# A decoder block on one Trainium2 core: the up projection as Strassen's seven products, the down projection in two passes

## The chip, the cores and the metric

The kernel runs on one core of a Trainium2 chip. Five engines work side by side and meet at semaphores: TensorE (PE in the profile; its weight loads are listed as PEld), VectorE (DVE), ScalarE (ACT), GpSimd (POOL) and SyncE (SP), which here only issues DMAs. The metric is the device time of one execution in microseconds (us). Lower is better.

## The reference

One block, 512 tokens, width 2048, all in float32:

```python
h = _rmsnorm(x, norm1_g[l]) * (1.0 + sc1) + sh1
p = h @ w_in[l]
...
mix = jnp.concatenate([y_rwkv, y_pool], axis=-1) @ w_out[l]
x = x + gt1 * mix
h = _rmsnorm(x, norm2_g[l]) * (1.0 + sc2) + sh2
x = x + gt2 * _conv_ffn(h, w_up[l], conv_w[l], conv_b[l], w_down[l])
return _rmsnorm(x, norm_f_g)

def _conv_ffn(h, w_up, conv_w, conv_b, w_down):
    T = h.shape[1]
    u = h @ w_up
    up = jnp.pad(u, ((0, 0), (CONV_WIDTH - 1, 0), (0, 0)))
    y = conv_b
    for j in range(CONV_WIDTH):
        y = y + conv_w[j] * up[:, j:j + T]
    val, gate = jnp.split(y, 2, axis=-1)
    return (jax.nn.silu(gate) * val) @ w_down
```

y_rwkv is a recurrent mixer over 16 heads, y_pool a causal mean over 2 to 16 tokens; w_up is 2048 x 11264, w_down 5632 x 2048. The six vectors sh1 to gt2 come from `silu(c) @ w_ada + b_ada`. The change touches the feed-forward part and what stands just ahead of it.

## The kernel before, in words

Features lie on the 128 partitions and tokens along the free dimension, so a tile is 128 features x 512 tokens. D = 2048 is 16 tiles (KT), the feed-forward width 5632 is 44 tiles (NF) for the value and 44 for the gate.

Every large matrix product keeps float32 precision with three matmuls in a 32-bit reduced format. `split_weights` (L102) loads 128 x 512 weights (256 KB) into `wraw`, ScalarE casts them to `whi`, and VectorE subtracts to get the remainder `wlo`. Activations are split in the same way (`split_act`, `modulate`). `mm3` (L111) then multiplies hi x hi, hi x lo and lo x hi into the same PSUM bank, at L112, L113 and L114. `project` (L116) does that over all tiles of the contracted dimension. There are three `whi` and three `wlo` buffers and four `wraw`.

Stage A (L166 to L683) holds the first norm, the input projection, the mixers and the first blocks of the output projection. Stage B begins at L688. The output projection's last six outputs are computed in two halves of 256 tokens (`out_half`), so that the second norm of the first half (`norm_rows`, `norm_bcast`, `second_norm`) runs while TensorE works on the second. The first two pairs of up tiles are also done in halves (`up_first`, L731).

Then come six groups of 8, 8, 8, 8, 4 and 8 pairs (GROUPS). A pair is a value tile and a gate tile: two `up_tile` products of 16 k-tiles x 3 matmuls with 512 columns each, a convolution straight from PSUM (`conv`, L818: one ScalarE and two VectorE instructions), silu, product and split into A. After a group's pairs its part of the down projection follows: 16 outputs, each of which VectorE scales with the gate and adds to `x2` in SBUF (L848). The last group's outputs 8 to 15 are done in halves, so that the final norm of the first half and its store (`finish`, L862) lie beside the second. `ada_gate2` (L804) computes the last sixteenth of the modulation, gt2, on VectorE during the first group, in 64 instructions with a 256 KB load each.

The order on each engine is laid out ahead of time by a scheduler that follows the order of the program text as a priority and takes what is ready by its own model; on the chip each engine then runs its list in order. All DMAs stand in SP's queue. A buffer (a tag with `bufs` slots) is used again when its readers are done. `GROUPS`, `H2` (the 16 split tiles of the second norm), `x2` (16 tiles of the residual) and `actp` are the names that the change removes or moves.

Of the kernel before, what the change touches and what calls it, by code (L numbers as in the profile page):

```python
# [16 lines left out]
P = 128  # L17
# [37 lines left out]
def block_kernel(ctx, tc, a, out, stop=None, dbg=None):  # L55
# [4 lines left out]
    actp = ctx.enter_context(tc.tile_pool(name="act", bufs=1))  # L60
    wp = ctx.enter_context(tc.tile_pool(name="wts", bufs=2))
# [3 lines left out]
    cmat = cp.tile([P, 5, P], F32, tag="cmat", name="cmat")  # L65
    nc.sync.dma_start(cmat, a["cmat"][:, :, :])
    ident, bones, bmean, cent, ones = (cmat[:, i, :] for i in range(5))
    masks = cp.tile([P, 4, P], F32, tag="masks", name="masks")
    nc.sync.dma_start(masks, a["mask4"][:, :, :])
    mlev = cp.tile([P, 2, 64], F32, tag="mlev", name="mlev")  # L70
    nc.sync.dma_start(mlev, a["mlev"][:, :, :])
    scanm = cp.tile([P, NC, 129], F32, tag="scanm", name="scanm")
    nc.gpsimd.memset(scanm, 1.0)
    nc.gpsimd.memset(scanm[:, :, 0:1], 0.0)
    lanei = cp.tile([64, 16, 16], F32, tag="lanei", name="lanei")
    nc.sync.dma_start(lanei, a["lanei"][:, :, :])
    prec = cp.tile([P, 16], F32, tag="prec", name="prec")
# [33 lines left out]
    def mm3(ps, wh, wl, xh, xl, start, stop):  # L111
        PE.matmul(ps, wh, xh, start=start, stop=False)  # L112
        PE.matmul(ps, wh, xl, start=False, stop=False)  # L113
        return PE.matmul(ps, wl, xh, start=False, stop=stop)  # L114
# [575 lines left out]
    HT = T // 2  # L690

# [6 lines left out]

    def sumsq(acc, src, lo, hi, fresh):
        if fresh:  # L700
            S.activation(acc[:, lo:hi], src, AF.Square)
        else:
            t = rb.tile([P, T], F32, tag="h2", name="sqx", bufs=2)
            S.activation(t[:, lo:hi], src, AF.Square)
            V.tensor_add(acc[:, lo:hi], acc[:, lo:hi], t[:, lo:hi])

    H2 = [(rb.tile([P, T], F32R, tag=f"hh{k}", name=f"hh{k}"), rb.tile([P, T], F32R, tag=f"hl{k}", name=f"hl{k}"))
          for k in range(KT)]

    def residual(f, ps, gate, acc, lo, hi, fresh):  # L710

        V.scalar_tensor_tensor(x2[f][:, lo:hi], ps, gate, x2[f][:, lo:hi], op0=ALU.mult, op1=ALU.add)
        sumsq(acc, x2[f][:, lo:hi], lo, hi, fresh)
# [11 lines left out]
    def second_norm(hf, rstd, k):  # L725
        hs = slice(hf * HT, (hf + 1) * HT)
        t = rb.tile([P, T], F32, tag="h2", name="h2", bufs=2)[:, 0:HT]
        hi, lo = H2[k]
        modulate(hi[:, hs], lo[:, hs], t, x2[k][:, hs], rstd, gsc2[:, k : k + 1], mod[:, 48 + k : 49 + k])

    def up_first(hf, k):  # L731
        hs = slice(hf * HT, (hf + 1) * HT)
        wh, wl = split_weights(a["wup0"][k, :, :], G if hf == 0 and k % 2 else V)
        for i in range(4):
            sl = slice(i * P, (i + 1) * P)
            mm3(ups[i][:, hs], wh[:, sl], wl[:, sl], H2[k][0][:, hs], H2[k][1][:, hs], start=k == 0, stop=k == KT - 1)

    acc = rb.tile([P, T], F32, tag="acc", name="acc")
    x2 = []
# [12 lines left out]
    for f in range(8):
        residual(f, pss[f], mod[:, 32 + f : 33 + f], acc, 0, T, f == 0)
    for f in range(8, NW):
        ps = bank()
        project(ps, a["wout"][f, :, :], M)
        residual(f, ps, mod[:, 32 + f : 33 + f], acc, 0, T, False)

    def out_half(hf, f, engs=(V,)):
        ps = bank()[:, 0:HT]  # L760
        project(ps, a["wout"][f, :, :], half(M, hf), engs=engs)
        residual(f, ps, mod[:, 32 + f : 33 + f], acc, hf * HT, (hf + 1) * HT, False)

    for f in range(NW, KT):
        out_half(0, f)
    for f in range(NW, KT):
        if f == NW + 1:
            dg = norm_rows(acc[:, 0:HT])
        if f == NW + 2:
            rstd0 = norm_bcast(dg)  # L770
        if f >= NW + 2:
            for k in range(3 * (f - NW - 2), 3 * (f - NW - 1)):
                second_norm(0, rstd0, k)
        out_half(1, f, (V, G) if f >= NW + 2 else (V,))

    ups = [bank() for _ in range(4)]
    for k in range(KT):
        if k + 12 < KT:
            second_norm(0, rstd0, k + 12)
        if k == 2:  # L780
            dg = norm_rows(acc[:, HT:T])
        if k == 5:
            rstd = norm_bcast(dg)
        if k >= 5:
            for k_ in range((k - 5) * 2, min((k - 4) * 2, KT)):
                second_norm(1, rstd, k_)
        up_first(0, k)
    for k in range(KT):
        up_first(1, k)
# [4 lines left out]
    def slot(i, dt=F32):  # L794
        return actp.tile([P, T], dt, tag=f"a{'hl'[i // 16]}{i % 16}", name="slot")

    cbs = []
    for i in range(4):
        t = slot(8 + i)
        nc.sync.dma_start(t, cact[0:1, i * T : (i + 1) * T].partition_broadcast(P))  # L800
        cbs.append(t)
    modg = cp.tile([P, 4, KT], F32, tag="modg", name="modg")

    def ada_gate2(j, after):  # L804
        for kq in range(4):
            wa = slot(12 + (4 * j + kq) % 4)
            nc.sync.dma_start(wa, a["ada2"][kq, 48 + j, :, :])
            jk = slot(24 + (4 * j + kq) % 2)
            with tc.issue_after(after.ins):
                V.scalar_tensor_tensor(jk, wa, 1.0, cbs[kq], op0=ALU.mult, op1=ALU.mult,  # L810
                                       accum_out=modg[:, kq, j : j + 1])

    def up_tile(n):
        ps = bank()
        project(ps, a["wup"][n, :, :], H2)
        return ps

    def conv(ps, j, tag):  # L818
        y = rb.tile([P, T], F32, tag=tag, name=tag, bufs=2)
        S.activation(y, ps, AF.Identity, bias=col("cb", j), scale=col("cw", 176 + j))  # L820
        V.scalar_tensor_tensor(y[:, 1:T], ps[:, 0 : T - 1], col("cw", 88 + j), y[:, 1:T], op0=ALU.mult, op1=ALU.add)
        V.scalar_tensor_tensor(y[:, 2:T], ps[:, 0 : T - 2], col("cw", j), y[:, 2:T], op0=ALU.mult, op1=ALU.add)
        return y

    j0 = 0
    for gi, gn in enumerate(GROUPS):
        A = []
        for jj in range(gn):
            j = j0 + jj
            yv = conv(ups[2 * j] if j < 2 else up_tile(2 * j), j, "t0")  # L830
            yg = conv(ups[2 * j + 1] if j < 2 else up_tile(2 * j + 1), 44 + j, "t1")
            S.activation(yg, yg, AF.Silu)
            after = V.tensor_mul(yv, yv, yg)
            A.append(split_act(jj, yv))
            if gi == 0 and jj >= 4:
                for i in range(4 * (jj - 4), 4 * (jj - 3)):
                    ada_gate2(i, after)
        if gi == 0:
            V.tensor_add(modg[:, 0, :], modg[:, 0, :], modg[:, 1, :])
            V.tensor_add(modg[:, 2, :], modg[:, 2, :], modg[:, 3, :])  # L840
            V.tensor_add(modg[:, 0, :], modg[:, 0, :], modg[:, 2, :])
            V.tensor_add(mod[:, 80:96], modg[:, 0, :], cols("b_ada", 80, 96))
        wsrc = a["wdn"][:, :, j0 * P : (j0 + gn) * P]
        if gi < len(GROUPS) - 1:
            for f in range(KT):
                ps = bank()
                project(ps, wsrc[f], A)
                V.scalar_tensor_tensor(x2[f], ps, mod[:, 80 + f : 81 + f], x2[f], op0=ALU.mult, op1=ALU.add)  # L848
        else:

            acc = rb.tile([P, T], F32, tag="acc", name="acc")

            def gate(f):
                return mod[:, 80 + f : 81 + f]

            def down_half(hf, f):
                ps = bank()[:, 0:HT]
                project(ps, wsrc[f], half(A, hf))
                residual(f, ps, gate(f), acc, hf * HT, (hf + 1) * HT, False)

            def finish(hf, k, rstd):
                hs = slice(hf * HT, (hf + 1) * HT)  # L862
                V.scalar_tensor_tensor(x2[k][:, hs], x2[k][:, hs], col("nf", k), rstd, op0=ALU.mult, op1=ALU.mult)  # L863
                nc.sync.dma_start(out[:, k, hs], x2[k][:, hs])
# [119 lines left out]
```

## Time and profile before

| | us |
|---|---|
| median of 3 runs (lowest to highest) | 2449.82 (2446.82 to 2450.76) |
| the profiled execution | 2452.14 |
| its span, first to last instruction | 2450.0 |
| TensorE matmul busy in it | 2347.1 |
| VectorE busy | 1408.7 |
| ScalarE busy | 874.6 |
| GpSimd busy | 23.7 |

The profile is of one execution. "Busy" joins overlapping instructions of an engine. Matmuls are pipelined, and their listed durations overlap, so how many start in a stretch tells more than their busy time. A group's row has the line, engine, operation, tiles (out<-in), shapes and count; then busy time and mean ns of one; then the engine's idle time ahead of it and who ended that. In a windows row each engine has its busy time and, in brackets, its number of instructions; then follow the granted TensorE clock, the DMA engines' share and GB/s.

### The profile page before, as it was taken

What the parts mean: (1) busy time and instruction counts of PE and PEld (TensorE: products, weight loads), DVE (VectorE), ACT (ScalarE), POOL (GpSimd) and SP (SyncE); (2) the same over time, 40 slices, a digit from 0 to 9 for tenths busy, and PEclk for the clock granted to TensorE, in tenths of its full rate; (3) what the DMA queues carried; (4) which work ended last, traced back from release to release, by engine and by line L of the source; (5) the groups of instructions that cost most, each with busy time, mean ns of one, the idle gap of its engine ahead of it and who ended that gap; (6) DMA issues with size and microseconds to landing.
All of it is one profiled execution on the core that took longest, in us unless ns stands there. A gap on an engine that the chain in (4) does not pass through costs nothing.

```text
span 2450.0 us, 36089 instructions
## 1 busy us (share of the span) xinstructions
PE 2347.1 (96%) x13714; PEld 1872.0 (76%) x13714; DVE 1408.7 (57%) x2698; ACT 874.6 (36%) x1402; POOL 23.7 (1%) x29
## 2 busy tenths in 40 slices
PE   4889999999999999999999999999999999999997
PEld 3656666667667889887888888888888888888887
DVE  7987677787774357757534443444344434444457
ACT  3244443443433336532223322333233323323333
POOL 0000000000000002100000000000000000000000
PEclk9999999999999999999999999999999999999999
DMA  9975564556662635538533333333332333332335
GB/s 353 337 233 152 166 185 140 163 162 178 169 200 85 203 111 185 181 113 260 161 96 98 96 98 95 99 96 98 95 99 95 99 95 99 95 99 95 99 97 174
DMA packets 232160, 352.61 MB, mean 144 GB/s; under 512 B 74865, under 2 KB 80177, under 8 KB 227761
## 3 DMA queue, kind: packets, MB, share of 16 engines
q1 hardware_dynamic: 231986, 350.30, 46.0%
q8 instruction: 107, 1.75, 0.3%
q14 instruction: 67, 0.55, 0.1%
HBM read 334.22 MB, written 16.00 MB: 143 GB/s over the span
## 4 chain that ended last, share of the span: by engine, by line
PE 68%; DMA 3%; DVE 2%; ACT 1%; issue 0%; SPq 0%; POOL 0%; DVEq 0%; ACTq 0%; POOLq 0%
PE b L112 20%; PE b L114 20%; PE b L113 20%; DMA wraw<-wup 1%; PE mm L112 1%; PE mm L113 1%; PE mm L114 1%; DMA war<-ada 0%; PE pa L290 0%; DMA slot<-ada 0%; DMA wraw<-wdn 0%; DVE wlo L108 0%; DVE x L863 0%; PE pa L114 0%; PE pa L113 0%
## 5 line engine op out<-in xcount | busy, mean ns | idle before, releaser
L108 DVE TENSOR_TENSOR wlo<-wraw,whi 128x512 fp32r<-128x512 f32 x772 | 533.2, 692 | 694.9 <-ACT whi L106 679.6
L106 ACT CAST whi<-wraw 128x512 fp32r<-128x512 f32 x788 | 489.3, 622 | 1229.0 <-PE b L113 925.2
L114 PE MATMUL b<-hh,wlo 128*128 128x512 f32 (+1 forms) x1472 | 561.2, 381 | 5.9 <-DVE wlo L108 5.0
L112 PE MATMUL b<-hh,whi 128*128 128x512 f32 (+1 forms) x1472 | 560.0, 380 | 0.0
L113 PE MATMUL b<-hl,whi 128*128 128x512 f32 (+1 forms) x1472 | 559.5, 380 | 0.0
L112 PE MATMUL b<-ah,whi 128*128 128x512 f32 (+1 forms) x992 | 353.4, 357 | 4.3 <-ACT whi L106 2.5
L114 PE MATMUL b<-ah,wlo 128*128 128x512 f32 (+1 forms) x992 | 351.9, 355 | 0.8 <-DVE wlo L108 0.8
L113 PE MATMUL b<-al,whi 128*128 128x512 f32 (+1 forms) x992 | 352.1, 355 | 0.0
L114 PEld LDWEIGHTS b<-hh,wlo 128*128 128x128 f32 x1472 | 277.0, 188 | 62.1 <-DVE wlo L108 8.5
L112 PEld LDWEIGHTS b<-hh,whi 128*128 128x128 f32 x1472 | 276.9, 188 | 52.9 <-ACT whi L106 0.5
L113 PEld LDWEIGHTS b<-hl,whi 128*128 128x128 f32 x1472 | 277.0, 188 | 52.3
L112 PEld LDWEIGHTS b<-ah,whi 128*128 128x128 f32 x992 | 187.5, 189 | 33.7 <-ACT whi L106 4.3
L113 PEld LDWEIGHTS b<-al,whi 128*128 128x128 f32 x992 | 187.6, 189 | 27.4 <-DVE al L134 1.1
L114 PEld LDWEIGHTS b<-ah,wlo 128*128 128x128 f32 x992 | 187.6, 189 | 26.8 <-DVE wlo L108 1.2
L112 PE MATMUL mm<-ah,whi 128*128 128x512 f32 x464 | 192.4, 415 | 6.3 <-ACT upad L257 5.5
L113 PE MATMUL mm<-al,whi 128*128 128x512 f32 x464 | 191.8, 413 | 0.0
L114 PE MATMUL mm<-ah,wlo 128*128 128x512 f32 x464 | 190.1, 410 | 0.0
L343 DVE SCALAR_TENSOR_TENSOR jkr<-war,cq 128x512 bf16<-128x512 f32 x192 | 131.3, 684 | 18.7 <-DMA war<-ada 15.9
L848 DVE SCALAR_TENSOR_TENSOR x<-b,mod,x 128x512 f32<-128x512 f32 x80 | 59.7, 750 | 111.4 <-PE b L114 111.3
L112 PEld LDWEIGHTS mm<-ah,whi 128*128 128x128 f32 x464 | 88.4, 190 | 35.1 <-issue 10.4
L113 PEld LDWEIGHTS mm<-al,whi 128*128 128x128 f32 x464 | 88.3, 190 | 29.3 <-issue 13.0
L114 PEld LDWEIGHTS mm<-ah,wlo 128*128 128x128 f32 x464 | 88.4, 191 | 23.8 <-issue 6.3
(259 smaller groups left out, 2282.0 us busy)
## 6 DMA issues: line engine op xcount, KB each, us to landing
wraw<-wup SPq DMA_DIRECT2D x368, 256.0 KB, 3.0
war<-ada SPq DMA_DIRECT2D x192, 256.0 KB, 3.4
wraw<-wdn SPq DMA_DIRECT2D x192, 256.0 KB, 2.7
wraw<-win SPq DMA_DIRECT2D x140, 256.0 KB, 4.0
wa<-ada SPq DMA_DIRECT2D x32, 1024.0 KB, 6.9
wraw<-wout SPq DMA_DIRECT2D x88, 256.0 KB, 3.0
slot<-ada SPq DMA_DIRECT2D x64, 256.0 KB, 3.7
sp<-spill SPq DMA_DIRECT2D x21, 256.0 KB, 2.7
```

The lines of the kernel that those rows point to most:

```text
L106: S.copy(hi, raw)
L108: eng.tensor_tensor(lo, raw, hi[:, :].bitcast(F32), op=ALU.subtract)
L112: PE.matmul(ps, wh, xh, start=start, stop=False)
L113: PE.matmul(ps, wh, xl, start=False, stop=False)
L114: return PE.matmul(ps, wl, xh, start=False, stop=stop)
L343: V.scalar_tensor_tensor(jk, wa, 1.0, cq[0], op0=ALU.mult, op1=ALU.mult, accum_out=modq[:, kq, j : j + 1])
L848: V.scalar_tensor_tensor(x2[f], ps, mod[:, 80 + f : 81 + f], x2[f], op0=ALU.mult, op1=ALU.add)
```

## The change

The up projection is done by Winograd's form of Strassen's algorithm, one level deep. Weights of one pair are a 2 x 2 block matrix: value and gate (w11, w12 of the value, w21, w22 of the gate) by the lower and upper half of the 2048 inputs, each quarter 128 x 1024 as it lies in SBUF. Activations are a 2 x 2 block matrix of lower and upper features by first and second 256 tokens. Seven products of quarters, 8 k-tiles x 3 matmuls with 256 columns each, replace eight. Four weight sums r1 to r4 for each pair are made on VectorE, every quarter or sum is split by `wsplit` (one ScalarE cast and one VectorE subtraction of 128 x 1024), and results are put together from PSUM with three adds and some copies. The activation sums T1 to T4 and Y11, Y21, Y22 are made once (`normed`, `combos`, `split4`): steps 0 and 1 of `combos` make a half of T1 each, steps 2 and 3 a half of T2, T3 and Y22 each and leave T4's sum in t2's place, all from the second norm, which lies in the four 1 MB buffers x2_0 to x2_3. `combos(n - 1)` follows `first_two(n)` for n from 1 to 4; T4 is split after the fifth. The pairs' two weight rows of 1 MB then go into x2_0 to x2_3 in turn. Since the second half of the tokens is late, the two products that need only the first half (w11 and w12 of the value) are computed ahead for the first NB = 5 pairs (`first_two`); their weights are loaded again later.

The gated activations go to DRAM (`ad`). The down projection runs in two passes of 22 tiles over all 16 outputs; `act_pair` loads the activations of a pass and splits them into the buffers of Y11 to T4 as these come free; results of the first pass go to DRAM (`yd`) and come back with x2, which also waits in DRAM (`x2d`). In the second pass outputs 8 to 15 are in halves. `ada_gate2` becomes 16 instructions on 1 MB each, two for each of the first eight outputs of the first pass. GpSimd no longer takes part in the splits. Constants of the mixers, `wts` and `act` lie in pools on the right side of SBUF and are closed ahead of the up projection; the pool `ub` takes their place.

```diff
+    hctx = ExitStack()
+    tp = hctx.enter_context(tc.tile_pool(name="tables", bufs=1, side="right"))
+    wp = hctx.enter_context(tc.tile_pool(name="wts", bufs=2, side="right"))
+    actp = hctx.enter_context(tc.tile_pool(name="act", bufs=1, side="right"))
...
+    def wide(name):
+        return rb.tile([P, 4, HT], F32, tag="wide", name=name, bufs=3)
+    def quad(i, name, dt=F32):
+        return rb.tile([P, 4, T], dt, tag=f"x2_{i}", name=name)
...
+    def out_done(f, ps, lo, hi):
+        residual(f, ps, mod[:, 32 + f : 33 + f], acc, lo, hi, f == 0)
+        nc.sync.dma_start(x2d[f][:, lo:hi], x2(f, slice(lo, hi)))
...
+    def normed(q, hs, rstd):
+        t = wide("xr")
+        V.tensor_tensor(t, x2q[q][:, :, hs], rstd[:, None, :].to_broadcast([P, 4, HT]), op=ALU.mult)
+        for i in range(4):
+            f = 4 * q + i
+            S.activation(x2(f, hs), t[:, i, :], AF.Identity, bias=mod[:, 48 + f : 49 + f], scale=gsc2[:, f : f + 1])
+    def split4(pool, tag, src):
+        t = pool.tile([P, 2, 4, HT], F32R, tag=tag, name=tag)
+        S.copy(t[:, 0, :, :], src)
+        V.tensor_tensor(t[:, 1, :, :], src, t[:, 0, :, :].bitcast(F32), op=ALU.subtract)
...
+    ub = ctx.enter_context(tc.tile_pool(name="ub", bufs=1, side="right", reuse_waits="tile"))
+    free = [(ub, f"s{i}") for i in range(NSLOT)]
...
+    def wsplit(src):
+        n = src.shape[-1]
+        hi = ub.tile([P, 2 * QW], F32R, tag="whi", name="uhi", bufs=3)
+        S.copy(hi[:, 0:n], src)
+        lo = ub.tile([P, 2 * QW], F32R, tag="wlo", name="ulo", bufs=3)
+        V.tensor_tensor(lo[:, 0:n], src, hi[:, 0:n].bitcast(F32), op=ALU.subtract)
+    def product(ps, w, Y, start=True):
+        wh, wl = wsplit(w)
+        for k in range(8):
...
+            mm3(ps, wh[:, sl], wl[:, sl], y[:, 0, k % 4, :], y[:, 1, k % 4, :], start=start and k == 0,
+                stop=k == 7, more=not start)
+    def row(n, pool, tag):
+        t = pool.tile([P, 4 * QW], F32, tag=tag, name="wrow")
+        nc.sync.dma_start(t, a["wup"][n, :, :])
+    def first_two(n):
+        w = row(2 * n, ub, f"t4{n % 2}")
...
+        product(ps, w[:, W1], Y11)
+        S.copy(s_[:, H1], ps)
+        product(ps, w[:, W2], Y21)
+        V.tensor_add(s_[:, H0], s_[:, H1], ps)
+    def combos(step):
+        if step in (0, 1):
+            normed(step, H1, rstd)
+            t = wide("t1")
+            V.tensor_sub(t, x2q[step][:, :, H0], x2q[step][:, :, H1])
+            T1[step] = split4(ub, f"t1{step}", t)
+        elif step in (2, 3):
+            g = step - 2
+            normed(g + 2, H1, rstd)
...
+    for n in range(NB):
+        first_two(n)
...
+    for g in range(2):
+        T4[g] = split4(ub, f"t4{g}", t4[g])
...
+    def finish_pair(j, u1, u2):
+        conv(u1.t, yv.t, col("cw", j), col("cw", 88 + j), col("cw", 176 + j), col("cb", j))
+        conv(u2.t, yg.t, ncw[:, 0, j : j + 1], ncw[:, 1, j : j + 1], ncw[:, 2, j : j + 1], col("cb", 44 + j))
+        S.activation(yg.t, yg.t, AF.Silu)
+        V.tensor_mul(yv.t, yv.t, yg.t)
+        nc.sync.dma_start(ad[j], yv.t)
+    def last_product(p):
+        j, u1, u2, b, w22, x = p
+        product(b, w22, T4, start=False)
...
+        finish_pair(j, u1, u2)
+    for j in range(NF):
...
+        if early:
+            u1 = ahead[j]
+            if pend:
+                last_product(pend)
+        else:
+            product(pa, w11, Y11)
+            S.copy(cap[:, H0], pa)
+            last_product(pend)
+            product(pb, w12, Y21)
+            V.tensor_add(u1[:, H0], cap[:, H0], pb)
+        V.tensor_add(r1, w21, w22)
+        product(pc, r1, T1)
+        S.copy(cap[:, H1], pc)
+        V.tensor_add(r2, r1, w11)
+        product(pa, r2, T2, start=early)
...
+        V.tensor_add(r4, r2, w12)
+        product(pc, r4, Y22, start=False)
+        V.tensor_add(u1[:, H1], cap[:, H0], pc)
+        V.tensor_add(r3, w11, w21)
...
+            product(pa, r3, T3, start=False)
+            V.tensor_add(u2[:, H1], cap[:, H1], pa)
...
+    def ada_gate2(i):
+        wa = quad(1 + i % 2, "wa2").rearrange("p a b -> p (a b)")
+        nc.sync.dma_start(wa, a["ada3"][i, :, :])
+        V.scalar_tensor_tensor(jk, wa, 1.0, cb, op0=ALU.mult, op1=ALU.mult, accum_out=mod[:, 80 + i : 81 + i])
+    def act_pair(i):
...
+    def down(ps, f, h, acts):
+        for k0 in range(0, NJ, 8):
+            w = wide("wd").rearrange("p a b -> p (a b)")
+            nc.sync.dma_start(w[:, 0 : n * P], a["wdn"][f, :, (h * NJ + k0) * P : (h * NJ + k0 + n) * P])
+            wh, wl = wsplit(w[:, 0 : n * P])
...
+    for f in range(KT):
+        down(ps, f, 0, A)
+        S.copy(s_.t, ps)
+        nc.sync.dma_start(yd[f], s_.t)
+        if f < 8:
+            ada_gate2(2 * f)
+            ada_gate2(2 * f + 1)
...
+    for f in range(NWF):
+        load_x2(f)
+        load_x2(f + NWF)
+        down(ps, f, 1, A)
+        residual(f, ps, gate(f), acc, 0, T, f == 0)
+    for f in range(NWF, KT):
+        down_half(0, f)
...
```

More of the change, by code (lines that the diff above doesn't have):

```diff
@@ L723, in norm_bcast @@
         return psb[:, 0:HT]
[L725 to L739, printed above, removed]
     for k0 in range(4, KT, 4):
@@ L767, in block_kernel @@
         if f == NW + 1:
-            dg = norm_rows(acc[:, 0:HT])
+            dg = norm_rows(acc[:, H0])
         if f == NW + 2:
-            rstd0 = norm_bcast(dg)
+            rstd = norm_bcast(dg)
         if f >= NW + 2:
[L772 to L787, printed above, removed]
@@ L788, in block_kernel @@
[L788 to L789 removed]
+            n = f - NW - 2
+            q = (0, 2, 1, 3)[n]
+            normed(q, H0, rstd)
+            (Y11, Y21)[q // 2][q % 2] = split4(rb, f"y{q}", x2q[q][:, :, H0])
+        out_half(1, f)
+    hctx.close()
     if stop == "B":
         return
[L794 to L801, printed above, removed]
```

297 lines of the change are left out of this document (190 added, 107 removed).

## The prediction

> **What bounds the kernel now.** I read the page's busy shares, slices and chain first. Then windows cut at the stages of the feed-forward part, for how many matmuls fit in a stretch. Then single rows for the price of each operation.
>
> ```profile
> span 2450.0 us, 36089 instructions
> ...
> PE 2347.1 (96%) x13714; PEld 1872.0 (76%) x13714; DVE 1408.7 (57%) x2698; ACT 874.6 (36%) x1402; POOL 23.7 (1%) x29
> ...
> PEclk9999999999999999999999999999999999999999
> ...
> PE 68%; DMA 3%; DVE 2%; ACT 1%; issue 0%; SPq 0%; POOL 0%; DVEq 0%; ACTq 0%; POOLq 0%
> PE b L112 20%; PE b L114 20%; PE b L113 20%; DMA wraw<-wup 1%; PE mm L112 1%; PE mm L113 1%; PE mm L114 1%; DMA war<-ada 0%; PE pa L290 0%; DMA slot<-ada 0%; DMA wraw<-wdn 0%; DVE wlo L108 0%; DVE x L863 0%; PE pa L114 0%; PE pa L113 0%
> ```
>
> The chain is the three matmuls of `mm3` (L112 to L114, 20% each) and nearly nothing else. "PE 96% busy" alone would not show it, since matmuls overlap. Counts do (columns PE, PEld, DVE, ACT, POOL, with instructions in brackets):
>
> ```profile
> core 0: us, PE busy (x) PEld busy (x) DVE busy (x) ACT busy (x) POOL busy (x), PEclk, DMA share, GB/s
> 920.00:970.00 50.00, 50.00 (x417) 49.95 (x417) 35.84 (x65) 30.01 (x55) 9.07 (x7) 1.00 0.56 176
> 975.00:1000.00 25.00, 23.61 (x182) 22.13 (x181) 22.51 (x44) 15.67 (x34) 9.50 (x8) 1.00 0.72 225
> 1100.00:1125.00 25.00, 24.94 (x109) 20.09 (x109) 19.80 (x47) 8.60 (x14) 0.00 (x0) 1.00 0.81 259
> 1125.00:1150.00 25.00, 22.66 (x99) 17.88 (x98) 19.24 (x46) 7.29 (x12) 0.00 (x0) 1.00 0.79 249
> 1150.00:1175.00 25.00, 22.07 (x89) 17.37 (x88) 19.35 (x47) 6.36 (x11) 0.00 (x0) 0.93 0.84 268
> 1600.00:2100.00 500.00, 500.00 (x2205) 413.27 (x2204) 212.33 (x306) 151.83 (x244) 0.00 (x0) 1.00 0.32 97
> 2400.00:2436.00 36.00, 32.31 (x258) 31.07 (x256) 27.88 (x60) 16.80 (x31) 0.00 (x0) 1.00 0.59 181
> 2436.00:2450.00 14.00, 1.30 (x6) 0.82 (x6) 7.59 (x21) 0.68 (x2) 0.00 (x0) 0.63 0.45 150
> ```
>
> From 1600 to 2100 us a matmul of 512 columns costs 500/2205 = 0.2268 us. From 920 to 970, where all have 256 columns, one costs 50/417 = 0.1199 us. Two halves cost 0.2398, 5.7% more than a whole. VectorE is 42% busy in the first stretch, 72% in the second. TensorE's pace is the limit here, so fewer columns through it is time saved, as long as its feeders keep up.
>
> **Term 1, matmul pace.** Up projection before: 88 tiles x 16 x 3 = 4224 matmuls, 192 of them cut in two halves: 4032 x 0.2268 + 384 x 0.1199 = 960.5 us. After: 44 pairs x 7 products x 8 x 3 = 7392 of 256 columns, 886.3 us: **-74.2**. (7/8 of the columns at 1.057 of the price is 0.925, so less than an eighth.) Down projection: the multiplications stay 2112, but with two passes the last eight outputs are cut in halves over 22 tiles, not 8. Before 1920 x 0.2268 + 384 x 0.1199 = 481.5; after 1584 x 0.2268 + 1056 x 0.1199 = 485.9: **+4.4**.
>
> Is 0.1199 safe at 7392 in a row? Each matmul brings its own weight load:
>
> ```profile
> 1000.10 0.28 PE L113 MATMUL b<-hl,whi 128*128 128x256 f32 x1
> 1000.10 0.19 PEld L114 LDWEIGHTS b<-hh,wlo 128*128 128x128 f32 x1
> 1000.22 0.28 PE L114 MATMUL b<-hh,wlo 128*128 128x256 f32 x1
> ```
>
> The load takes 0.19 us, starts with the matmul ahead of it, and the next matmul starts 0.12 later. Loads fill the window (49.95 of 50 us) and still don't set the pace. [...]
>
> **Term 2, stalls of before that go.** Expected matmul time against window: 975-1000 lacks 25 - 182 x 0.1199 = 3.2 us, the three windows from 1100 lack 0.3, 2.5 and 4.8, 2400-2436 lacks 36 - 258 x 0.1199 = 5.1. The first is the norm of the second half beside `up_first`; the middle three are `ada_gate2` with 64 loads beside the up weights; the last are short halves (24 matmuls, 2.9 us) late for weights:
>
> ```profile
> 1131.47 0.62 ACT L106 CAST whi<-wraw 128x512 fp32r<-128x512 f32 x1 [2.40 <-DMA wraw<-wup]
> 2425.20 0.62 ACT L106 CAST whi<-wraw 128x512 fp32r<-128x512 f32 x1 [1.76 <-DMA wraw<-wdn]
> ```
>
> All three structures are replaced. `ada_gate2` goes to the first down pass, two 1 MB loads for each of eight outputs; an output there has 66 x 0.2268 = 15.0 us of TensorE. Last halves become 66 matmuls, 7.9 us. Term: **-16** (bounds -16 and -10). The new costs at those places are terms 3 and 5.
>
> **Prices on VectorE and ScalarE.**
>
> ```profile
> L108 DVE TENSOR_TENSOR wlo<-wraw,whi 128x512 fp32r<-128x512 f32 x772 | 533.2, 692 | 694.9 <-ACT whi L106 679.6 <-PE mm L114 7.3 <-DMA war<-ada 2.0
> L204 DVE SCALAR_TENSOR_TENSOR jk<-wa,cb 128x2048 bf16<-128x2048 f32 x32 | 73.1, 2284 | 0.0
> L821 DVE SCALAR_TENSOR_TENSOR t<-b,vec,t 128x511 f32<-128x511 f32 x88 | 65.7, 749 | 0.0
> L833 DVE TENSOR_TENSOR t<-t,t 128x512 f32<-128x512 f32 x44 | 30.1, 685 | 0.8 <-ACT t L832 0.8
> L705 DVE TENSOR_TENSOR acc<-acc,sqx 128x256 f32<-128x256 f32 x28 | 11.7, 419 | 2.5 <-ACT sqx L704 2.5
> L712 DVE SCALAR_TENSOR_TENSOR x<-b,mod,x 128x256 f32<-128x256 f32 x28 | 13.5, 483 | 7.6 <-PE b L114 7.1
> ```
> ```profile
> L106 ACT CAST whi<-wraw 128x512 fp32r<-128x512 f32 x788 | 489.3, 622 | 1229.0 <-PE b L113 925.2 <-PE mm L113 125.0 <-issue 38.4
> L820 ACT ACTIVATE t<-b,vec 128x512 f32<-128x512 f32 x88 | 67.9, 776 | 0.0
> L832 ACT ACTIVATE t<-t 128x512 f32<-128x512 f32 x44 | 27.6, 628 | 1.7 <-DVE t L822 1.7
> L704 ACT ACTIVATE sqx<-x 128x256 f32<-128x256 f32 x28 | 11.7, 417 | 4.1 <-DVE x L712 3.8
> L172 ACT ACTIVATE cb<-cb 128x2048 f32<-128x2048 f32 x1 | 1.9, 1909 | 8.6 <-DMA cb<-c 8.6
> ```
> ```profile
> 1191.32 0.75 DVE L848 SCALAR_TENSOR_TENSOR x<-b,mod,x 128x512 f32<-128x512 f32 x1 [1.22 <-PE b L114]
> 1191.99 0.68 DVE L108 TENSOR_TENSOR wlo<-wraw,whi 128x512 fp32r<-128x512 f32 x1
> ```
>
> The new width is 1024. Between 512 and 2048 VectorE adds (2284 - 692)/1536 = 1.04 ns per element: 692 + 531 = 1.22 us. ScalarE: 622 + 512 x (1909 - 622)/1536 = 1.05 us. An independent VectorE instruction starts 0.08 us before its predecessor ends (0.67 apart, 0.75 long).
>
> **Term 3, a late pair** (39 of them). TensorE: 7 x 24 x 0.1199 = 20.1 us, 2.88 per product. VectorE: 7 `lo` parts and 4 weight sums, 11 x 1.22 = 13.4; four convolution steps 3.0; product 0.69; three adds from PSUM at 0.42, 1.3: 18.4 us, and 16.9 with the overlap of 0.08 on 19 instructions. ScalarE: 7 casts 7.4, four copies 1.7, two convolution starts 1.6, silu 0.6: 11.2. So VectorE becomes 84 to 91% busy, TensorE still the longer. Three `whi`/`wlo` buffers let the `lo` of product n+3 start when n ends, 5.8 us before it is needed; sums depend only on rows that are loaded a pair ahead; copies of a bank that is added to again have one product, 2.88 us, for 0.42. Behind a late instruction on VectorE stand the next `lo`, and TensorE waits for that. Bounds: 0 (the 920-970 window, VectorE 72%, lacks nothing) and 13% of 20.1 = 2.6 us a pair (975-1000: VectorE 22.51 of 25 us, 3.2 us lost). In that window a weight group lasted only 12 matmuls, 1.4 us, and VectorE and ScalarE took turns on each norm tile, so I take a value near the lower end, 0.2 us: **+8**.
>
> **Term 4, the start of the up projection.** Ten products run ahead (28.8 us of TensorE) while VectorE makes 10 `lo`, 5 adds and, in `combos` and T4, 22 operations of 1024: 32 x 1.22 + 2.1 = 41.1, or 38 with overlap. TensorE idles 9 to 12 for that. The rows of pair 0 (1 MB) go into tags that `combos` reads to its last step, so load, sum, cast and `lo` may follow it:
>
> ```profile
> wa<-ada SPq DMA_DIRECT2D x32, 1024.0 KB, 6.9
> ...
> 2440.10 7.70 SPq L864 DMA_DIRECT2D out<-x  x16
> ```
>
> 6.9 + 1.22 + 1.05 + 1.22 = 10.4, partly beside the last six operations of VectorE (7.3): idle 9 to 20, taken 15. The five early pairs have 5 products (14.4 us) against 9 x 1.22 + 3.7 + 4 x 0.42 = 16.4 on VectorE (15.0 with overlap): 3 to 10, taken 5. The first row lands in space that the closing pools give up at the end of the output projection: 0 to 9, taken 4. **+24** (12 to 39).
>
> **Term 5, edges.** Last output halves: 4 x 0.69 + 0.48 + 0.42 + 2 x 1.22 = 6.1 us VectorE against 48 x 0.1199 = 5.8, no GpSimd now: **+2** (0 to 3). Up to down: 22 activations come back from DRAM; VectorE needs 0.69 + 1.22/8 = 0.84 us per tile, TensorE uses one in 0.68, so 22 x 0.16 = 3.5 late: **+4** (0 to 10). Between the passes 16 of 22 tiles come into buffers that the last output of pass one frees pair by pair (1.36 us each), three pairs ahead of their use: each is wanted 15.0 + 2 x 1.36 = 17.7 us after its buffer is free, for a load, two casts and two `lo`: 0. The second norm overwrites x2 in place and waits for x2's write to DRAM, of outputs long done: 0. `ada_gate2` (2 x 2.37 us VectorE per 15.0 of TensorE), the 22 writes of x2 (7.70/16 = 0.48 us of SP each, over some 100 us), 44 writes and reads of activations, `yd`: 0, covered by TensorE; SP issues fewer loads than before (2 rows per pair, not 8). The end after the last matmul (14 us) stays.
>
> **Sum.** -74.2 + 4.4 - 16 + 8 + 24 + 2 + 4 = -47.8. The profiled execution took 2452.1 us (span 2450.0): 2404. It was 2.3 above the median of the runs shown: **2402**.
>
> **Rivals.**
> A. VectorE sets the late pair (slower). Place: in-order queue between weight sums, `lo` parts and the convolution of the pair before. For it: 975-1000, where 90% VectorE went with 13% lost. Against: 920-970. At that loss, 39 x 2.6 = 102 in place of 8: about 2496. It decides from 20.1 + (47.8 + 8)/39 = 21.5 us per pair. Between: 0.6 to 1 us a pair, 2418 to 2433.
> B. The start is hidden (VectorE runs the sums earlier, rows come early): terms 4 and 5 at their lower ends and term 3 at 0: 2452 - 69.8 - 16 + 12 - 2.3 = 2376. For it: 920-970 makes norm tiles for the next stage too and loses nothing. Against: 41 us of VectorE beside 28.8 of TensorE.
> C. Weight loads don't hide in the long run: 7392 x 0.19 = 1404, some 520 more, near 2920. Against: the three rows of term 1, and 417 matmuls in 50 us. [...]
>
> **How the numbers follow.** My forecast 0.60 (own range 2386 to 2417), A's full form 0.13, its milder form 0.13, B 0.13, C 0.01. Range 2376 to 2446 leaves out A, C and a little: 2 in 10 at most. A change of 0.2%, 5 us, is about what a measurement of this kernel can tell. Slower: A, C and the tail of the milder form, 0.16; same 0.03; faster 0.81.
>
> **What would show it.** Right: pairs of 20.1 to 20.5 us after the first 150 us of the stage, some 208 matmuls per 25 us; VectorE near 85%; one idle stretch of 10 to 20 us on TensorE at the end of `combos`; no DMA wait in the last 40 us. Wrong: TensorE waiting for `lo` in every pair, matmuls of 256 at more than 0.12 us, or gaps at the pass borders over 10 us.

## The result, and the profile after

| | us |
|---|---|
| before, median of 4 runs (lowest to highest) | 2450.29 (2446.82 to 2451.16) |
| after, median of 4 runs (lowest to highest) | 2518.82 (2516.07 to 2522.28) |
| ratio after / before, 95% interval | 1.0283 (1.0264 to 1.0302) |
| the profiled execution of after, its span | 2522.28, 2520.5 |

The changed kernel is slower by 2.8%; 2402 us was forecast. The two profiled spans differ by 70.5 us. The page of the kernel after, its head, TensorE's slices, the clock's slices and the chain:

```profile
span 2520.5 us, 42054 instructions
...
PE 2324.0 (92%) x17026; PEld 2001.5 (79%) x17026; DVE 1735.1 (69%) x2709; ACT 1043.0 (41%) x1466; POOL 2.7 (0%) x13
...
PE   4879999999999999799999999999999999988776
...
PEclk9999999999999999899999999999999999999988
...
PE 63%; DVE 6%; DMA 2%; ACT 2%; issue 1%; SPq 0%; ACTq 0%; DVEq 0%
PE b L123 19%; PE b L121 18%; PE b L122 18%; DVE ulo L839 2%; ACT uhi L837 1%; PE mm L121 1%; PE mm L123 1%; PE mm L122 1%; DVE x L737 1%; DVE x L1070 0%; DMA al<-ad 0%; DMA war<-ada 0%; PE pa L299 0%; PE pa L122 0%; PE pa L121 0%
```

TensorE's busy time fell by 23 us and the span grew by 70, so the change put idle time where there was none. The slices say where: one 7 in the middle (the start of the up projection), and 8, 8, 7, 7, 6 at the end. The clock drops in the same two places. VectorE's share of the chain rose from 2% to 6%, and two of its new lines are `ulo` (L839, the split of weights) and `x` (L737, `residual`). Windows by stage (PE, PEld, DVE, ACT, POOL with instructions in brackets; granted clock, DMA share, GB/s):

```profile
core 0: us, PE busy (x) PEld busy (x) DVE busy (x) ACT busy (x) POOL busy (x), PEclk, DMA share, GB/s
1018.00:1036.00 18.00, 0.99 (x7) 0.79 (x6) 16.81 (x16) 9.10 (x11) 0.00 (x0) 0.60 0.59 203
1036.00:1136.00 100.00, 97.52 (x788) 96.50 (x788) 96.98 (x116) 50.89 (x60) 0.00 (x0) 0.97 0.41 146
1200.00:1800.00 600.00, 600.00 (x5006) 600.00 (x5005) 517.59 (x568) 316.33 (x417) 0.00 (x0) 1.00 0.33 119
1903.00:1923.00 20.00, 16.55 (x55) 11.99 (x56) 18.74 (x25) 10.28 (x17) 0.00 (x0) 0.83 0.96 332
1923.00:2150.00 227.00, 227.00 (x990) 185.48 (x989) 88.65 (x89) 62.16 (x80) 0.00 (x0) 1.00 0.64 208
2300.00:2400.00 100.00, 77.31 (x534) 72.59 (x533) 34.36 (x40) 25.31 (x32) 0.00 (x0) 0.93 0.39 111
```

The up projection does what it was to do: 5006 matmuls in 600 us, 0.1199 us each. The first pass of the down projection too: 990 in 227 us, 0.2293 each. The second pass, from about 2150, does not: 534 halves in 100 us where 0.1199 allows 834, with VectorE 34% and ScalarE 25% busy and DMA at 39%. TensorE idles there, and so does everything that could feed it. Its need is 8 x 66 x 0.2268 + 16 x 66 x 0.1199 = 246.4 us; it ran from 2153.2 to 2505.4 us, 106 more. The waits of PE in the second pass (engine, line, what it waited for: us in total, times, longest us):

```profile
PE b L121 <- ACT uhi L837: 53.7, 22, 7.9
PE b L123 <- DVE ulo L839: 14.9, 23, 0.8
```

The pass has 24 outputs and so 23 borders, and there is a pair of waits at all of them but the first: the first matmul waits for the first cast of its weights, and its third for their `lo` part. (Outputs 0 and 1 overlap, since activations are still arriving; output 0 also squares straight into `acc`.) The timeline around one border between two outputs shows why (start, us, engine or queue, line, operation; in brackets idle time ahead and what ended it; matmuls without a wait left out):

```profile
2331.61 0.48 DVE L737 SCALAR_TENSOR_TENSOR x<-b,mod,x 128x256 f32<-128x256 f32 x1 [4.50 <-PE b L123]
2332.19 0.42 ACT L731 ACTIVATE sqx<-x 128x256 f32<-128x256 f32 x1 [6.07 <-DVE x L737]
2332.51 1.98 ACT L837 CAST uhi<-wd 128x1024 fp32r<-128x1024 f32 x2
2332.64 0.42 DVE L732 TENSOR_TENSOR acc<-acc,sqx 128x256 f32<-128x256 f32 x1 [0.54 <-ACT sqx L731]
...
2333.58 2.36 DVE L839 TENSOR_TENSOR ulo<-wd,uhi 128x1024 fp32r<-128x1024 f32 x2 [0.51 <-ACT uhi L837]
2333.60 0.38 PE L121 MATMUL b<-act,uhi 128*128 128x256 f32 x1 [2.02 <-ACT uhi L837]
...
2334.86 0.39 PE L123 MATMUL b<-act,ulo 128*128 128x256 f32 x1 [0.76 <-DVE ulo L839]
```

Read the ScalarE rows first. It was idle for 6.07 us until the residual of output f (`x`) was there, squared it, and only then cast two weight blocks of output f+1, back to back. It did not wait for them: the load of the first was issued at 2324.77, and the loads of this stretch landed 3.2 to 3.7 us after their issue, some 4 us ahead of the cast. VectorE's list has the same order: residual, addition of the square, then `lo`. Both engines ran their lists in order here, ScalarE idle for those 6.07 us with the weights there, and the lists put the end of output f ahead of the weights of output f+1. So such a border costs the residual (0.48), the square (0.42), a cast (1.03, the median of this pass) and a `lo` (1.22) in series. In the kernel before, the residual of an output half stands behind the first `lo` of the next one:

```profile
2394.78 0.69 DVE L108 TENSOR_TENSOR wlo<-wraw,whi 128x512 fp32r<-128x512 f32 x1 [0.41 <-ACT whi L106]
...
2395.64 0.48 DVE L712 SCALAR_TENSOR_TENSOR x<-b,mod,x 128x256 f32<-128x256 f32 x1 [0.17 <-PE b L114]
```

The residual is in the change's `residual` and `sumsq`. In the second pass `sumsq` writes its square to a tile `sqx` with the tag `wide`, and this tag's three buffers are also those of the weights `wd` in `down`. In before `sqx` had two buffers of a tag (`h2`) that holds no weights.

### The profile page after: what moved, and what is told of

It is laid out like the page before. It is cut to its first block, busy times and chain, and to the rows that moved or that the text cites. A ratio compares the mean times of both kernels' runs of the same rounds, so it can differ in the third digit from the quotient of the medians.

```text
span 2520.5 us, 42054 instructions
## 1 busy us (share of the span) xinstructions
PE 2324.0 (92%) x17026; PEld 2001.5 (79%) x17026; DVE 1735.1 (69%) x2709; ACT 1043.0 (41%) x1466; POOL 2.7 (0%) x13
## 4 chain that ended last, share of the span: by engine, by line
PE 63%; DVE 6%; DMA 2%; ACT 2%; issue 1%; SPq 0%; ACTq 0%; DVEq 0%
PE b L123 19%; PE b L121 18%; PE b L122 18%; DVE ulo L839 2%; ACT uhi L837 1%; PE mm L121 1%; PE mm L123 1%; PE mm L122 1%; DVE x L737 1%; DVE x L1070 0%; DMA al<-ad 0%; DMA war<-ada 0%; PE pa L299 0%; PE pa L122 0%; PE pa L121 0%
## 5 line engine op out<-in xcount | busy, mean ns | idle before, releaser
L121 PE MATMUL b<-t,uhi 128*128 128x256 f32 x1408 | 399.7, 284 | 20.7 <-ACT uhi L837 18.5
L123 PE MATMUL b<-t,ulo 128*128 128x256 f32 x1408 | 399.4, 284 | 1.0 <-DVE ulo L839 0.9
L122 PE MATMUL b<-t,uhi 128*128 128x256 f32 x1408 | 399.1, 283 | 0.0
L121 PE MATMUL b<-act,uhi 128*128 128x512 f32 (+1 forms) x880 | 319.4, 363 | 57.2 <-ACT uhi L837 55.5
L123 PE MATMUL b<-act,ulo 128*128 128x512 f32 (+1 forms) x880 | 320.0, 364 | 15.5 <-DVE ulo L839 15.5
L122 PE MATMUL b<-act,uhi 128*128 128x512 f32 (+1 forms) x880 | 317.3, 361 | 0.2 <-DVE act L1016 0.2
L121 PE MATMUL b<-y,uhi 128*128 128x256 f32 x1056 | 298.4, 283 | 2.4 <-ACT uhi L837 2.4
L122 PE MATMUL b<-y,uhi 128*128 128x256 f32 x1056 | 299.4, 284 | 0.0
L123 PE MATMUL b<-y,ulo 128*128 128x256 f32 x1056 | 299.0, 283 | 0.0
L121 PEld LDWEIGHTS b<-t,uhi 128*128 128x128 f32 x1408 | 270.9, 192 | 21.8 <-ACT uhi L837 19.0
L123 PEld LDWEIGHTS b<-t,ulo 128*128 128x128 f32 x1408 | 270.9, 192 | 1.7 <-DVE ulo L839 1.6
L122 PEld LDWEIGHTS b<-t,uhi 128*128 128x128 f32 x1408 | 270.8, 192 | 0.0
L839 DVE TENSOR_TENSOR ulo<-r,uhi 128x1024 fp32r<-128x1024 f32 x176 | 215.1, 1222 | 74.7 <-ACT uhi L837 74.7
L114 ACT CAST whi<-wraw 128x512 fp32r<-128x512 f32 x228 | 141.0, 620 | 298.6 <-PE mm L122 121.7
L839 DVE TENSOR_TENSOR ulo<-wd,uhi 128x1024 fp32r<-128x1024 f32 (+1 forms) x120 | 134.1, 1135 | 157.2 <-ACT uhi L837 157.2
L116 DVE TENSOR_TENSOR wlo<-wraw,whi 128x512 fp32r<-128x512 f32 x228 | 156.3, 688 | 119.2 <-ACT whi L114 102.0
```

The costliest lines, as they stand in the source:

```text
L114: S.copy(hi, raw)
L116: eng.tensor_tensor(lo, raw, hi[:, :].bitcast(F32), op=ALU.subtract)
L121: PE.matmul(ps, wh, xh, start=start, stop=False, skip_group_check=more)
L122: PE.matmul(ps, wh, xl, start=False, stop=False, skip_group_check=more)
L123: return PE.matmul(ps, wl, xh, start=False, stop=stop, skip_group_check=more)
L839: V.tensor_tensor(lo[:, 0:n], src, hi[:, 0:n].bitcast(F32), op=ALU.subtract)
```

## The experiments

Line numbers of the experiments' kernels are up to eight above those of after. Theory: the order of the two lists costs the time, and the `sqx` tile among the weight buffers brings that order about. First rival: the square on ScalarE costs it, by two more hand-overs between engines and by its place in ScalarE's queue. Second rival: it is the number of buffers, since two are left for three weight chunks and loads come late.

**The square in a buffer of its own.**

```diff
-            t = wide("sqx")[:, 0:2, :].rearrange("p a b -> p (a b)")
+            own = sq_slot[0]("sqx") if sq_slot else None
+            t = own.t if own else wide("sqx")[:, 0:2, :].rearrange("p a b -> p (a b)")
             S.activation(t[:, lo:hi], src, AF.Square)
             V.tensor_add(acc[:, lo:hi], acc[:, lo:hi], t[:, lo:hi])
+            if own:
+                own.done()
...
     acc = Slot("acc").t
+    sq_slot.append(Slot)
```

> In the second down pass the square of the final norm gets a buffer of its own (one of the 512-wide slots) and no longer shares the three `wide` buffers with the weights. Theory S (the shared buffer makes the order on ScalarE and VectorE put the residual of one output ahead of the next output's weight splits): the second pass loses its 2.66 + 0.7 us per full output and 2.2 + 0.9 per half, some 100 us in all: about 2415 us. Rival Q (the square itself, which stands in ScalarE's queue and waits for the last matmul, holds the casts back whatever its buffer): 2510 to 2520. Rival A of the prediction (VectorE sets the time): no change, 2519.

Measured: 2415.75 us (2412.35 to 2416.74), ratio to before 0.985 (0.983 to 0.9871). The kernel is now 1.5% faster than before. The last stretch of the table above, in this kernel:

```profile
2300.00:2400.00 100.00, 98.60 (x822) 98.34 (x820) 56.24 (x81) 39.95 (x50) 0.00 (x0) 1.00 0.62 181
```

822 halves in 100 us, where after had 534. From its first matmul with a `lo` weight to its last matmul the down projection takes 500.7 us in place of 602.2: 101.5 of the lost time. ScalarE and VectorE beside the halves:

```profile
2324.32 1.05 ACT L842 CAST uhi<-wd 128x1024 fp32r<-128x1024 f32 x1 [1.83 <-PE b L122]
2325.40 1.23 DVE L844 TENSOR_TENSOR ulo<-wd,uhi 128x1024 fp32r<-128x1024 f32 x1 [1.65 <-ACT uhi L842]
2326.44 0.84 ACT L842 CAST uhi<-wd 128x768 fp32r<-128x768 f32 x1 [1.07 <-PE b L122]
2326.56 0.48 DVE L742 SCALAR_TENSOR_TENSOR x<-b,mod,x 128x256 f32<-128x256 f32 x1
2327.18 0.41 ACT L734 ACTIVATE sqx<-x 128x256 f32<-128x256 f32 x1
```

Casts now wait for TensorE to free a `whi` buffer (`<-PE b L122`), that is, they run ahead, and the residual comes behind casts and a `lo` of the next output. Both the theory and the second rival allow this result.

**The square on VectorE, in the shared buffer.**

```diff
-            S.activation(t[:, lo:hi], src, AF.Square)
+            if sq_dve:
+                V.tensor_mul(t[:, lo:hi], src, src)
+            else:
+                S.activation(t[:, lo:hi], src, AF.Square)
```

> The square of the second pass is made on VectorE, its buffer stays one of the shared three; ScalarE's queue then holds nothing that waits for the last matmul. Theory S: VectorE's own queue still has the residual ahead of the next `lo`, so the loss stays: 2500 to 2530 us. Rival Q: the loss goes, about 2415.

Measured: 2510.02 us in one run; the span is 12.3 us below that of after, most of the loss stays. ScalarE has no part in the end of an output any more, and its casts are done early, but VectorE's list still holds the next `lo` back:

```profile
2335.70 0.48 DVE L742 SCALAR_TENSOR_TENSOR x<-b,mod,x 128x256 f32<-128x256 f32 x1 [5.41 <-PE b L123]
2336.22 0.42 DVE L734 TENSOR_TENSOR sqx<-x 128x256 f32<-128x256 f32 x1
2336.68 0.42 DVE L737 TENSOR_TENSOR acc<-acc,sqx 128x256 f32<-128x256 f32 x1
2337.02 2.35 DVE L844 TENSOR_TENSOR ulo<-wd,uhi 128x1024 fp32r<-128x1024 f32 x2
2338.30 0.58 PE L123 MATMUL b<-act,ulo 128*128 128x256 f32 x1 [2.40 <-DVE ulo L844]
```

The first rival falls: without ScalarE the wait moves from `uhi` to `ulo` and is as long, 2.40 us.

**The buffers stay shared, the residual comes later in the program text.** The residual of output f is emitted behind the weight split of output f+1's second chunk.

```diff
+    late = []
...
+            if k0 and late:
+                late.pop()()
...
-        residual(f, ps, gate(f), acc, 0, T, f == 0)
+        late.append(lambda f=f, ps=ps: residual(f, ps, gate(f), acc, 0, T, f == 0))
```

> The shared buffer stays, but in the program's text the residual of an output stands behind the weight splits of the next output's first two chunks. Theory S in the form that it is the order that costs, not the number of buffers: most of the loss goes, 2410 to 2440 us. If three buffers are simply too few for weights and square: 2490 to 2520.

Measured: 2420.93 us (2415.41 to 2422.32), ratio 0.987 (0.9851 to 0.9889). Its halves:

```profile
2300.00:2400.00 100.00, 95.58 (x782) 93.88 (x780) 54.99 (x78) 39.16 (x48) 0.00 (x0) 1.00 0.58 182
```

782 of 834, with the same three buffers as after. So the second rival explains at most the 40 matmuls by which this falls short of 822, and the order is the cause of the rest. Why the scheduler lays that order when the tag is shared, and not when the square has its own buffer, was not shown; the lists only show that it does.

**How close VectorE is to the pace in a late pair.** The prediction's rival A was not borne out, and VectorE's 518 of 600 us says that some 2.8 us a pair are free. To measure the edge, additions of 128 x 512 whose result is used nowhere were put into each pair, on top of the first experiment: four, then eight.

```diff
         V.tensor_mul(yv.t, yv.t, yg.t)
+        for _ in range(4):
+            V.tensor_add(yg.t, yg.t, yv.t)
```

> e1_own_slot with four more VectorE additions of 512 for each of the 44 pairs, whose result nobody reads (0.61 us each, 2.44 per pair). The profile of the changed kernel has VectorE busy 17.3 us of a 20.1 us late pair, so 2.76 free. If only the sum counts, late pairs stay at 20.1 us and only the five early pairs, which VectorE already limits, get longer: +12 us against e1_own_slot. If the order of the queue needs the free time: up to 2.4 us for each of 39 pairs, +95.

> e1_own_slot with eight more VectorE additions of 512 per pair (4.9 us), twice those of e7_four_more_on_vector, whose late pairs stayed at 20.1 us with VectorE busy 578 of 600 us. VectorE then has 17.3 + 4.9 = 22.2 us per late pair. If it takes the lead as soon as its sum is longer than TensorE's: late pairs of 22.2 to 22.5 us, 39 x 2.1 to 2.4 = +82 to 94, early pairs +24: 2520 to 2535. If it still hid: below 2460.

Measured, one run each: 2432.1 us with four, 2523.12 with eight. The late pairs with four and with eight:

```profile
1200.00:1800.00 600.00, 600.00 (x5006) 600.00 (x5005) 578.06 (x686) 316.86 (x419) 0.00 (x0) 1.00 0.33 118
```
```profile
1200.00:1800.00 600.00, 562.82 (x4527) 556.70 (x4526) 588.05 (x731) 287.40 (x378) 0.00 (x0) 0.98 0.30 107
```

At 96% VectorE still costs TensorE nothing: 5006 matmuls, as without. With eight a pair takes 600/4527 x 168 = 22.3 us: VectorE's own sum (17.3 + 8 x 0.6) is then above 20.1 and sets the pair. So the time passes from one engine to the other somewhere between 96% and the crossing of their sums; no loss was seen ahead of it. The 16.6 us that four cost in the span lie elsewhere: 8.4 in the early pairs (750 matmuls from 1040 to 1140 in place of 820), 1.3 ahead of the up projection, the rest behind the late pairs, where I did not follow it further.

**Can the start of the up projection be shortened?** Five kernels, all on the first experiment. First, a sixth pair ahead:

```diff
-NB = 5
+NB = 6
```

> e1_own_slot with NB = 6: six pairs' first two products run ahead, so TensorE has 34.4 us of work, not 28.7, beside the sums of activations. If VectorE's sums are what TensorE waits for (17.2 us idle), the idle stretch shrinks by 5.7 less the two `lo` and one add that come on top (2.8): 2412 to 2413. If TensorE waits for pair 0's rows, which follow the last sum: no change, 2415 to 2417.

Measured: 2413.0 us (2410.9 to 2415.74), ratio 0.9846 (0.9831 to 0.9862), the lowest of all; but the interval overlaps that of the first experiment, and the ratios (0.985 there) are only 1 us apart, so a gain is not shown. TensorE's one idle stretch of 17.2 us became two, of 4.7 and 6.9. Of the 5.6 us saved, some 3.5 went to matmuls at half pace behind the gaps (some 6 us of it from 980 to 1200, against 2 to 3 in the first experiment; the last section tells of them).

Then GpSimd takes work off VectorE, in the last four output halves (first diff) or for the `lo` parts of Y22 and T4 (second):

```diff
-        out_half(1, f)
+        out_half(1, f, (V, G) if f >= NW + 2 else (V,))
```

> e1_own_slot with every second `lo` of the last four output halves on GpSimd, as in the kernel before. There the stage from the first output in bank b to the up projection took 92 us, in the changed kernel 97. If the missing GpSimd is the reason: -3 to -5 us, 2411 to 2413. If it is the norm in one piece of 1024 (VectorE, four ScalarE instructions, VectorE) ahead of the weights in the queue: less than 1 us.

```diff
-            Y22[g] = split4(ub, f"y22{g}", x2q[g + 2][:, :, H1])
+            Y22[g] = split4(ub, f"y22{g}", x2q[g + 2][:, :, H1], G)
...
-        T4[g] = split4(ub, f"t4{g}", t4[g])
+        T4[g] = split4(ub, f"t4{g}", t4[g], G)
```

> e1_own_slot with the `lo` parts of Y22 and T4 (four of 128 x 1024) on GpSimd. VectorE has 4 x 1.22 = 4.9 us less to do ahead of pair 0. If VectorE's total is the limit there: -3 to -5 us, 2411 to 2413. If GpSimd slows VectorE or is itself late (a 512-wide `lo` took it 1.25 us before, so some 2.5 here): 0 to +5.

Measured: 2417.19 us (2416.59 to 2418.47), ratio 0.9864 (0.9848 to 0.9881), no gain; and 2420.58 (2419.77 to 2420.91), ratio 0.9876 (0.9861 to 0.9891). In the second TensorE's idle stretch is 20 us, not 17. VectorE and GpSimd in it:

```profile
1023.08 3.25 DVE L888 SCALAR_TENSOR_TENSOR t<-t,x 128x1024 f32<-128x1024 f32 x1
...
1031.93 1.22 DVE L970 TENSOR_TENSOR r<-wrow 128x1024 f32<-128x1024 f32 x1
1033.18 3.42 DVE L975 TENSOR_TENSOR r<-r,wrow 128x1024 f32<-128x1024 f32 x1
```
```profile
1022.80 2.45 POOL L795 TENSOR_TENSOR t<-t,t 128x1024 fp32r<-128x1024 f32 x1 [7.94 <-ACT t L794]
...
1033.17 2.35 POOL L795 TENSOR_TENSOR t<-t,t 128x1024 fp32r<-128x1024 f32 x1 [4.63 <-ACT t L794]
```

A VectorE operation that takes 1.22 us alone took 3.42 when it started with GpSimd's: it ended 1.08 us after GpSimd did (1033.17 + 2.35), so, estimated from these times, it stood still nearly all the while. The work that GpSimd took over came back as waiting. (GpSimd's 512-wide `lo` took 1.31 us in the mean in before, where the expectation has 1.25.)

Last, all of these together, with `ada_gate2` held behind the weight splits; and the sixth pair with that hold alone:

```diff
-        V.tensor_tensor(lo[:, 0:n], src, hi[:, 0:n].bitcast(F32), op=ALU.subtract)
+        last_lo[:] = [V.tensor_tensor(lo[:, 0:n], src, hi[:, 0:n].bitcast(F32), op=ALU.subtract)]
...
-        V.scalar_tensor_tensor(jk, wa, 1.0, cb, op0=ALU.mult, op1=ALU.mult, accum_out=mod[:, 80 + i : 81 + i])
+        with tc.issue_after(last_lo[0].ins):
+            V.scalar_tensor_tensor(jk, wa, 1.0, cb, op0=ALU.mult, op1=ALU.mult, accum_out=mod[:, 80 + i : 81 + i])
```

> The three edits above together, and `ada_gate2` held behind the weight split that precedes it in the text (one of its 2.29 us stood ahead of an addition that TensorE waited for, 1.9 us). If the gains add: -10 to -14, 2402 to 2406 us. If they share one cause, as much as the largest: 2410 to 2413.

> e4_six_ahead with `ada_gate2` held behind the weight split that precedes it in the text, without GpSimd. If the 2.29 us of it ahead of the last pair's addition is what TensorE waits for at the border of up and down: -2, 2410 to 2412. If the activations coming back from DRAM are: no change, 2412 to 2415.

Measured: 2420.55 us (2419.95 to 2425.6), ratio 0.9881 (0.9864 to 0.9898), and 2414.95 (2413.05 to 2421.45), ratio 0.9862 (0.984 to 0.9884). The hold took 0.8 us off the wait that it was meant for (`u`), and the waits for activations (`act`) grew by 3.6. Waits of PE with six ahead alone, then with the hold:

```profile
PE b L121 <- ACT act L1020: 2.1, 2, 1.4
...
PE b L121 <- DVE u L995: 1.2, 1, 1.2
...
PE b L122 <- DVE act L1021: 1.0, 1, 1.0
```
```profile
PE b L121 <- ACT act L1023: 4.5, 2, 3.7
PE b L122 <- DVE act L1024: 2.2, 1, 2.2
...
PE b L121 <- DVE u L997: 0.4, 1, 0.4
```

So 2413 us stays the best time, 1.5% below before; the kernels of this series whose times lie 1 to 3 us from each other are not told apart.

## Why the prediction was wrong, point by point

**The step that failed** is term 5, with the half of term 1 on which it rests. The second pass was costed at TensorE's pace, 485.9 us for both passes, and what ends an output was not in any term: `residual` and `sumsq`, which this pass calls 24 times, were given no cost and no cover was named. In before the same two calls end the outputs of the last group, and their rows stand in the prediction as prices (0.483, 0.419 and 0.417 us), but not as a chain that can stand ahead of the next output's weights. The change puts `sqx` and `wd` into one tag; the prediction does not mention it and did not ask what order would follow. Measured: 106 us, of which some 100 came back with the first experiment. No rival held it either: A put its slower case into the up projection.

The price of one such wait was also more than the wait. Adding up, over the second pass, what each matmul's start was late beyond 0.1199 or 0.2268 us gives some 77 us of gaps and 27 us of matmuls at half pace behind them (some records are missing). The half pace is in the last section. Of the 77 us, 8 are one stop at 2426.9 that a late load ended; it too is gone in the first experiment.

**The rest of the sum, against its terms.**

- Term 1, matmul pace: right. 0.1199 us held over 5006 matmuls in a row, with weight loads busy in 600 of 600 us. Rival C is out.
- Term 2, stalls of before that go: those of `ada_gate2` in the up projection and of the norm beside `up_first` are gone with their code. Those of the last halves did not go; the second pass brought longer ones.
- Term 3, late pairs: forecast +8, measured 0 (5006 x 0.1199 = 600.2). The 17.3 us of VectorE per pair lie within the 16.9 to 18.4 of the forecast, and the estimates of 1.22 and 1.05 us for 1024 columns were exact:

```profile
L839 DVE TENSOR_TENSOR ulo<-r,uhi 128x1024 fp32r<-128x1024 f32 x176 | 215.1, 1222 | 74.7 <-ACT uhi L837 74.7
L837 ACT CAST uhi<-r 128x1024 fp32r<-128x1024 f32 x176 | 185.2, 1052 | 192.1 <-PE b L122 171.4
```

  What was wrong is the reason for a loss: VectorE, not the longest engine, cost nothing here at 86%, and at 96% neither. The stretch 975-1000 of before, from which rival A took its 13%, is no measure of that: TensorE's four waits there, 0.3 to 0.5 us each, are for a `lo`, two of VectorE's and two of GpSimd's.
- Term 4, the start: forecast +24, measured some 28: one idle stretch of 17.2 us with VectorE busy in 16.81 of 18 us (forecast 15), 100 - 788 x 0.1199 = 5.5 us in the hundred that follow (forecast 5), and some 5 between the last output half and the idle stretch (forecast 4), of which 2.7 are waits of the first matmuls. At the first of these the cast of the new weights stands behind the square of the last output, as in the second pass. Right in size, but the 5.5 were not VectorE behind its pace in five pairs: 1.8 are one gap at 1036.0, a wait for the cast of pair 0's second weight sum, and 2.3 the half clock behind it (granted 0.50 from 1036 to 1042).
- Term 5, edges: the output halves cost 5.4 us more than before, forecast +2. From up to down some 10 us, forecast +4: 2.2 us because an addition stood behind an `ada_gate2` of 2.29 us on VectorE, and 20 - 55 x 0.2268 = 7.5 us while activations came back, with DMA at 96%:

```profile
1895.83 2.29 DVE L1003 SCALAR_TENSOR_TENSOR jk<-wa,cb 128x2048 bf16<-128x2048 f32 x1
1898.04 0.42 DVE L979 TENSOR_TENSOR u<-cap,b 128x256 f32<-128x256 f32 x1
...
1898.98 0.41 DVE L990 TENSOR_TENSOR u<-cap,b 128x256 f32<-128x256 f32 x1
...
1899.45 0.39 PE L121 MATMUL b<-t,uhi 128*128 128x256 f32 x1 [2.22 <-DVE u L990]
```

  `ada_gate2` was costed at 0, "covered by TensorE". On VectorE that cover did not hold for what stood behind it in the list: the addition at 1898.04 began as the 2.29 us of `ada_gate2` ended. The steady part of the first pass lost 227 - 990 x 0.2268 = 2.5 us, the border between the passes nothing to speak of.
- The first output in bank `b` of the profiled run also began 5 us later than before (887.0 against 882.0), in work that the change leaves as it was but for the pools. In the experiments' kernels, which are the same up to there, it began at 879.2 to 886.1, so I give this no cause; the spans compared here carry some 7 us of this scatter.

From -47.8: late pairs -8, output halves +3.4, start +4, up to down +6, first pass +2.5, the late begin +5, second pass +106: 71 us, against 70.5 in the spans. With the one order undone, the first experiment gave 2415.75, within 14 us of the 2402 forecast.

The prediction's signs: pairs of 20.1 us, VectorE near 85% (86%) and one idle stretch of 10 to 20 us at the end of `combos` came. "No DMA wait in the last 40 us" held for TensorE, whose waits there are for `uhi`, `ulo` and the norm; but earlier, at 2426.9, it stood for 8 us, with 14 `out` stores of `finish` in SP's queue ahead of weight loads. "Gaps at the pass borders over 10 us" looked for the loss at the wrong border: it came at nearly every output, some 3 us at a time and more with the half pace behind it.

## What to carry to other kernels

Where stages follow each other on in-order engines, cost the end of one work item against the beginning of the next: list what each feeding engine has to do for item f's end and for item f+1's start, and ask which stands first. A small scratch tile in a tag that also holds prefetched weights is a reason to ask, since the order of the lists can then change at no sign in the program text; a buffer of its own, or emitting the ending later, gave back 100 us here. VectorE, busy 86 and 96% beside a longer TensorE, cost nothing here (5006 matmuls in 600 us both times); ScalarE and VectorE, 25 and 34% busy with their lists in the wrong order, did (534 matmuls in 100 us, 822 in the first experiment).

## What was not expected of the hardware

Short gaps cost TensorE more than their length here. The two waits of the border shown above, 2.02 and 0.76 us with two matmuls between them, were followed by a stretch at a granted clock of 0.50; the kernel after, windows of 2 us behind that border:

```profile
2334.00:2336.00 2.00, 1.24 (x9) 1.15 (x9) 1.94 (x2) 0.49 (x1) 0.00 (x0) 0.91 0.75 197
2336.00:2338.00 2.00, 2.00 (x11) 2.00 (x10) 0.71 (x1) 0.83 (x1) 0.00 (x0) 0.50 0.43 98
2338.00:2340.00 2.00, 2.00 (x14) 2.00 (x14) 0.25 (x1) 0.00 (x0) 0.00 (x0) 0.73 0.77 209
```

From 2335.66 to 2339.07, 3.41 us, the matmuls start 0.21 us apart and not 0.12: another 1.5 us lost. It came behind every waiting border of the whole outputs (seven) and behind every second one of the halves. Apart from the stop at 2426.9 no single wait of this pass was longer than 2.5 us, so it took no idle stretch as long as the half clock itself. The trace shows the edge: the clock's changes lie whole multiples of 3.41 us apart (2188.89, 2209.36, 2335.66), and the stretch of this length ahead of this half clock (2332.25 to 2335.66) has TensorE busy 1.31 us, 38%. The border at 2320, with the same two waits, falls across two such stretches (from 2318.59 and from 2322.01) with 1.79 and 2.27 us, 52% and 67%, and no half clock followed. Cut in this way, the trace of after has 451 stretches at full clock from 880 us on: the 19 with TensorE busy 47% or less were all followed by 0.50, and none of the 432 with 48% or more. The edge is not the same everywhere: ahead of 880 us a stretch with 1.84 us, 54% (from 570.97), was followed by 0.50, and in before one with 1.60 us, 47% (from 2426.10), was not. The busy time is as the profile models it. Why the clock goes down was not shown.

GpSimd beside VectorE, in the run with the `lo` parts of Y22 and T4 on GpSimd: the addition that takes 1.22 us alone took 3.42 beside a GpSimd subtraction of 2.35, and the operation at 1023.08, whose like takes 1.22 in after (L883), took 3.25 beside one of 2.45 and the start of the next. Why was not shown.
